# Four of eight pair steps in seven products, with two of their four weight sums made by accumulating DMAs

## The chip, the cores and the metric

One core of one Trainium2 chip runs the whole kernel. The metric is the device time of one execution in microseconds (us). The core has five engines: TensorE (PE, matrix products; PEld is its weight load), VectorE (DVE), ScalarE (ACT), GpSimd (POOL) and SyncE (SP, which here only issues DMAs). Each engine works through its own queue in order.

## The reference

One hybrid decoder layer on 256 tokens of width 2048, all in float32:

```
x = x + 1/2 * SwiGLU_1(RMSNorm(x))          # 2048 -> 5632 -> 2048
x = x + W_out [ GLA(u) ; MoBA(u) ]          # u = RMSNorm(x) @ W_in
x = x + CrossAttn(RMSNorm(x), RMSNorm(mem))
x = x + 1/2 * SwiGLU_2(RMSNorm(x))
swiglu(h) = (silu(h @ w_gate) * (h @ w_up)) @ w_down
```

The change touches only `h @ w_gate` and `h @ w_up` of the two SwiGLU blocks.

## The kernel before, in words

**Three products for one.** Float32 accuracy is had from products of a rounded type: `split_to` (L151) makes of every operand a rounded part "hi" (ACT, L152) and a rest "lo" (DVE, L153), and `mm3` (L163) issues three matmuls, hi*hi, hi*lo and lo*hi (L165 to L167). Activations are stationary (128x128), weights move (128x512). Split weights live in the buffers `whi` and `wlo`, six of each (`HIS`), each 128x2x512.

**Pairs.** A SwiGLU block has 11 column blocks of 512. The first is done plainly (`Block`), the other ten by the class `Pair`, so there are 20 pairs in the kernel. A pair computes gate and up for both halves of the tokens in eight steps, q = 0 to 7. A step loads one raw tile of 1 MB, `raw[:, 0:4]` (`load_pair`, L144: two DMAs of 512 KB on SP): places 1 and 2 hold two 128-row blocks of gate weights, places 0 and 3 two of up weights. Seven PSUM banks collect the products p1, r6, r7, p2, r5, r3, q4, and the last adds on DVE (`early`, `gates`, `ups`) turn them into the four results. `KINDS` gives the kind of each step:

- An N step splits the gate blocks and the up blocks (two `whi`/`wlo` buffers) and makes eight products of three matmuls each.
- An S step makes seven products of three matmuls each. Besides the gate blocks and one up block it needs four sums of weights, made by DVE in two tiles "st" (L232 to L235), and their splits: four `whi`/`wlo` buffers in all.

`KINDS = "NSNSNSNN"`, so steps 1, 3 and 5 are S. After the last S step, `early` (L246) takes p1, r6 and r7 out of PSUM; after step 7, `gates` and `ups` take out the others. `half_kb` tiles (`T2K` = 7 of 2 KB) hold these. `Normed.sums` (L369) prepares, once per SwiGLU block, the combined activations of each step ("eh"/"el" for S, "dh"/"dl" for N).

**What sets the order.** The text of the kernel is not the order of the queues. The framework's planner, at build time, orders each engine's queue by its own estimate of when things are ready, and sets the waits; buffers of one tag are handed out again when their last reader is done. So the sums of an S step may stand in DVE's queue well before that step's splits. Raw tiles have three buffers (`RAWS`), released when the last of a step's readers is done. POOL has nothing to do in the SwiGLU blocks.

Of the kernel before, what the change touches and what calls it, by code (L numbers as in the profile page):

```python
# [2 lines left out]

# [10 lines left out]
ALU = mybir.AluOpType  # L14
# [3 lines left out]
P = 128  # L18
# [6 lines left out]
NB = 512  # L25
# [19 lines left out]
OFF_MV = OFF_MK + BH * DH  # L45
RAWS = 3
HIS = 6
T2K = 7
KINDS = "NSNSNSNN"


@with_exitstack
def hymba_layer(ctx: ExitStack, tc: tile.TileContext, x, mem, ffn1_norm, ffn1_w_gate, ffn1_w_up,
# [3 lines left out]
    nc = tc.nc  # L57
# [10 lines left out]
    pools = {}  # L68
# [13 lines left out]
    def nm(s):  # L82
        count[0] += 1
        return f"{s}_{count[0]}"
# [35 lines left out]
    def own_tile(shape, tag, dtype=F32):  # L120
        return pools["own"].tile(shape, dtype, tag=tag, name=nm(tag))

    def tmp_tile(shape, tag, bufs=2, dtype=F32):
        return pools["tmp"].tile(shape, dtype, tag=tag, name=nm(tag), bufs=bufs)

    def half_kb(shape=(P, NB)):
        return tmp_tile(list(shape), "t2k", 8 if "mix" in pools else T2K)

    ahead = {}

    def raw_tile():
        return wp.tile([P, 4, NB], F32, tag="raw", name=nm("raw"))

    def load_raw(k0, c0, w, n=NB, step=4):

        raw = raw_tile()[:, :step, :n]
        nc.sync.dma_start(raw, w[k0 * P:(k0 + step) * P, c0:c0 + n].rearrange("(k p) n -> p k n", p=P))
        return raw

    def take_raw(k0, c0, w, n=NB, step=4):  # L140
        key = id(w), k0, c0
        return ahead.pop(key) if key in ahead else load_raw(k0, c0, w, n, step)

    def load_pair(k0, c0, wg, wu):  # L144

        raw = raw_tile()
        for dst, w in ((raw[:, 1:3, :], wg), (raw[:, 0:4:3, :], wu)):
            nc.sync.dma_start(dst, w[k0 * P:(k0 + 2) * P, c0:c0 + NB].rearrange("(k p) n -> p k n", p=P))
        return raw

    def split_to(hi, lo, src):  # L151
        nc.scalar.activation(hi, src, AF.Copy)  # L152
        nc.vector.tensor_tensor(lo, src, hi.bitcast(F32), op=ALU.subtract)  # L153

    def split_raw(raw):

        k, n = raw.shape[1:]
        bufs = 3 if "mix" in pools else HIS
        hi, lo = (tmp_tile([P, 2, NB], tag, bufs, F32R)[:, :k, :n] for tag in ("whi", "wlo"))
        split_to(hi, lo, raw)  # L160
        return [(hi[:, i, :], lo[:, i, :]) for i in range(k)]
# [7 lines left out]
    def bank(n=NB):  # L169
        return pools["mm"].tile([P, NB], F32, tag="mm", name=nm("mm"))[:, :n]  # L170

    class Block:
# [7 lines left out]
        def step(self, k0, nk=4):  # L180
            hi, lo = self.a
            k2 = k0
            while k2 < k0 + nk:
                raw = take_raw(self.w_k0 + k2, self.c0, self.w, self.n, min(4, k0 + nk - k2))
                for i in range(0, raw.shape[1], 2):
                    ws = split_raw(raw[:, i:i + 2])
                    for t in range(NT):
                        s = slice(t * P, (t + 1) * P)
                        for k, w in enumerate(ws, k2 + i):
                            mm3(self.ps[t], (hi[:, k, s], lo[:, k, s]), w, k == 0,  # L190
                                k == self.nk - 1)
                k2 += raw.shape[1]
            pump()
            if k0 + nk == self.nk:
                self.done(self.ps)

    class Pair:
# [3 lines left out]
        def __init__(self, a, wg, wu, c0):  # L201
            self.a, self.wg, self.wu, self.c0 = a, wg, wu, c0
            self.p = {n: bank() for n in ("p1", "r6", "r7", "p2", "r5", "r3", "q4")}
            self.left = {n: KINDS.count("S") + (0 if n in ("p1", "r6", "r7") else 1) *
                         KINDS.count("N") for n in self.p}
            self.total = dict(self.left)
# [11 lines left out]
        def step(self, q):  # L218
            if self.begun is None:
                self.begun = set()  # L220
            a = self.a
            raw = load_pair(2 * q, self.c0, self.wg, self.wu)
            g, u2 = raw[:, 1:3], raw[:, 3:4]
            if KINDS[q] == "N":
                gs, us = split_raw(g), split_raw(raw[:, 0:4:3])
                for name, t, ws in (("p2", 0, gs), ("q4", 1, gs), ("r3", None, us), ("r5", 1, us)):
                    for i, w in enumerate(ws):
                        x = a.diff(2 * q + i) if t is None else a.plain(t, 2 * q + i)
                        self.add(name, x, w, i == 1)
            else:  # L230
                sa, sb = (tmp_tile([P, 2, NB], "st") for _ in range(2))
                nc.vector.tensor_tensor(sa, raw[:, 1:4:2], raw[:, 0:1].to_broadcast([P, 2, NB]),  # L232
                                        op=ALU.add)
                nc.vector.tensor_tensor(sb[:, 0:1], sa[:, 0:1], u2, op=ALU.add)
                nc.vector.tensor_tensor(sb[:, 1, :], sb[:, 0, :], raw[:, 2, :], op=ALU.add)  # L235
                gs, (us,) = split_raw(g), split_raw(u2)
                sums = split_raw(sa) + split_raw(sb)
                e, o = 2 * q, 2 * q + 1
                for name, x, w in (("p1", a.plain(0, e), gs[0]), ("p2", a.plain(0, o), gs[1]),
                                   ("r3", a.comb(3, q), us),  # L240
                                   ("r5", a.comb(0, q), sums[0]), ("r7", a.comb(2, q), sums[1]),
                                   ("r6", a.comb(1, q), sums[2]), ("q4", a.plain(1, o), sums[3])):
                    self.add(name, x, w, True)
            pump()

# [28 lines left out]
    def pump():  # L274

        while behind:
            try:
                next(behind[0])
                return
            except StopIteration:  # L280
                behind.popleft()
# [60 lines left out]
    class Normed:  # L342
# [6 lines left out]
        def begin(self):  # L349
            self.hi, self.lo = (act_tile([P, KC, T], tag, F32R) for tag in ("xhi", "xlo"))  # L350
            self.ss = small.tile([P, NT, 4], F32, tag="ss", name=nm("ss"))
            if self.pairs:
                self.s = [q for q in range(KC // 2) if KINDS[q] == "S"]
                self.n = [q for q in range(KC // 2) if KINDS[q] == "N"]
                self.e = [own_tile([P, len(self.s), 4, P], t, F32R) for t in ("eh", "el")]
# [13 lines left out]
        def sums(self, q, x):  # L369

            f = tmp_tile([P, 4, P], "xg", 3)
            if KINDS[q] == "S":
                for out, x0, x1 in ((f[:, 0], x[1][:, 0], x[1][:, 1]),
# [633 lines left out]
```

## Time and profile before

| | |
|---|---|
| median of 2 runs | 1957.38 us (1956.18 to 1958.57) |
| the profiled execution, device time | 1955.91 us |
| its span, first to last instruction | 1954.2 us |
| PE busy | 1933.9 us, 99% of the span |
| DVE busy | 1410.2 us, 72% |
| ACT busy | 1019.8 us, 52% |
| POOL busy | 23.8 us, 1% |
| granted TensorE clock | 1.00 |
| read from memory | 365.50 MB |

The profile is of one execution. Busy time is the time in which an engine had an instruction in work; matmuls overlap each other at their ends, so PE's busy time shows that it never rests, and the pace is read from the starts of successive matmuls. A wait is put down to what released it.

### The profile page before, as it was taken

The page shows a single profiled execution, that of the slowest core. Times are in us where ns is not written, and L with a number is a line of the kernel's source. Part 1 is how long each engine was busy: PE and PEld are TensorE (multiplying, and loading weights), DVE is VectorE, ACT ScalarE, POOL GpSimd, SP SyncE. Part 2 cuts the span into 40 slices and gives each one's busy share as a digit, 9 for nine tenths or more (in the row PEclk, how much of TensorE's full clock was granted, in tenths as well). Part 3 has the DMA queues.
Part 4 walks back from the last instruction along what each step waited for, and adds up shares of the span by engine and source line. Part 5 has one row for each costly group of instructions (what it writes and reads, how often), then busy time and mean ns, then how long its engine had stood idle before and what let it go on. Part 6 is the DMA issues. An engine that isn't in the chain of part 4 may idle for free.

```text
span 1954.2 us, 23322 instructions
## 1 busy us (share of the span) xinstructions
PE 1933.9 (99%) x8932; PEld 1604.1 (82%) x8932; DVE 1410.2 (72%) x1726; ACT 1019.8 (52%) x1268; POOL 23.8 (1%) x52
## 2 busy tenths in 40 slices
PE   7999999999999999999999999999999999999999
PEld 6888888888888888987788888888888888888887
DVE  7788569895589755465665766979856988558873
ACT  6555445554355545635464655655534555435552
POOL 0000000000000000000000000000000000000000
PEclk9999999999999999999999999999999999999999
DMA  7565555565556636554455544656555565655663
GB/s 239 203 206 193 195 191 185 204 207 202 194 173 214 205 126 205 172 192 148 152 172 200 178 160 152 207 181 214 194 194 185 184 213 196 211 196 172 205 206 128
DMA packets 192456, 369.13 MB, mean 189 GB/s; under 512 B 8692, under 2 KB 19144, under 8 KB 192344
## 3 DMA queue, kind: packets, MB, share of 16 engines
q1 hardware_dynamic: 192344, 367.64, 56.0%
q8 instruction: 70, 1.15, 0.2%
q14 instruction: 42, 0.34, 0.0%
HBM read 365.50 MB, written 2.10 MB: 188 GB/s over the span
## 4 chain that ended last, share of the span: by engine, by line
PE 97%; DVE 1%; DMA 1%; ACT 0%; issue 0%; SPq 0%
PE mm L165 31%; PE mm L167 31%; PE mm L166 31%; PE aux L415 1%; PE aux L328 1%; DVE wlo L153 0%; DMA raw<-in_xattn_w_o_dram 0%; PE aux L746 0%; DMA raw<-in_ffn_w_gate_dram 0%; ACT whi L152 0%; PE aux L696 0%; PE aux L691 0%; PE aux L667 0%; PE aux L932 0%; PE aux L781 0%
## 5 line engine op out<-in xcount | busy, mean ns | idle before, releaser
L153 DVE TENSOR_TENSOR wlo<-raw,whi 128x1024 fp32r<-128x1024 f32 (+3 forms) x704 | 807.7, 1158 | 433.0 <-ACT whi L152 429.0
L152 ACT ACTIVATE whi<-raw 128x1024 fp32r<-128x1024 f32 (+3 forms) x704 | 698.1, 1003 | 778.7 <-PE mm L167 720.3
L165 PE MATMUL mm<-whi,xhi 128*128 128x512 f32 (+2 forms) x1356 | 528.0, 390 | 1.2 <-ACT whi L152 1.2
L166 PE MATMUL mm<-wlo,xhi 128*128 128x512 f32 (+2 forms) x1356 | 522.5, 385 | 0.7 <-DVE wlo L153 0.7
L167 PE MATMUL mm<-whi,xlo 128*128 128x512 f32 (+2 forms) x1356 | 522.2, 385 | 0.0
L167 PE MATMUL mm<-whi,biglo 128*128 128x512 f32 x864 | 336.8, 390 | 0.1
L165 PE MATMUL mm<-whi,bighi 128*128 128x512 f32 x832 | 326.3, 392 | 0.0
L166 PE MATMUL mm<-wlo,bighi 128*128 128x512 f32 x832 | 324.1, 390 | 0.0
L165 PEld LDWEIGHTS mm<-whi,xhi 128*128 128x128 f32 x1356 | 254.8, 188 | 51.0 <-ACT whi L152 2.2
L167 PEld LDWEIGHTS mm<-whi,xlo 128*128 128x128 f32 x1356 | 254.7, 188 | 50.3 <-DVE xlo L153 0.5
L166 PEld LDWEIGHTS mm<-wlo,xhi 128*128 128x128 f32 x1356 | 255.1, 188 | 48.6 <-DVE wlo L153 1.3
L167 PEld LDWEIGHTS mm<-whi,biglo 128*128 128x128 f32 x864 | 162.1, 188 | 34.5 <-DVE biglo L153 0.6
L166 PEld LDWEIGHTS mm<-wlo,bighi 128*128 128x128 f32 x832 | 156.3, 188 | 31.7
L165 PEld LDWEIGHTS mm<-whi,bighi 128*128 128x128 f32 x832 | 156.2, 188 | 31.5
L153 DVE TENSOR_TENSOR wlo<-st,whi 128x1024 fp32r<-128x1024 f32 x120 | 146.6, 1222 | 30.3 <-ACT whi L152 26.8
L152 ACT ACTIVATE whi<-st 128x1024 fp32r<-128x1024 f32 x120 | 127.2, 1060 | 66.0 <-PE mm L167 43.4
L165 PE MATMUL mm<-whi,eh 128*128 128x512 f32 x240 | 93.4, 389 | 0.0
L167 PE MATMUL mm<-whi,el 128*128 128x512 f32 x240 | 93.4, 389 | 0.0
L166 PE MATMUL mm<-wlo,eh 128*128 128x512 f32 x240 | 93.4, 389 | 0.0
L232 DVE TENSOR_TENSOR st<-raw 128x1024 f32<-128x1024 f32 x60 | 73.2, 1220 | 7.0 <-DMA raw<-in_ffn_w_up_dram 6.3
L165 PE MATMUL mm<-whi,dh 128*128 128x512 f32 x200 | 77.8, 389 | 0.0
L166 PE MATMUL mm<-wlo,dh 128*128 128x512 f32 x200 | 77.8, 389 | 0.0
(206 smaller groups left out, 1422.8 us busy)
## 6 DMA issues: line engine op xcount, KB each, us to landing
raw<-in_ffn_w_down_dram SPq DMA_DIRECT2D x88, 1024.0 KB, 5.1
raw<-in_ffn_w_gate_dram SPq DMA_DIRECT2D x162, 512.0 KB, 3.9
raw<-in_ffn_w_up_dram SPq DMA_DIRECT2D x160, 512.0 KB, 4.8
raw<-in_w_in_dram SPq DMA_DIRECT2D x40, 1024.0 KB, 5.1
raw<-in_w_out_dram SPq DMA_DIRECT2D x16, 1024.0 KB, 5.1
raw<-in_ffn_w_up_dram SPq DMA_DIRECT2D x8, 1024.0 KB, 5.2
raw<-in_ffn_w_gate_dram SPq DMA_DIRECT2D x7, 1024.0 KB, 5.2
raw<-in_w_in_dram SPq DMA_DIRECT2D x8, 688.0 KB, 4.2
```

What stands on the lines that cost most here:

```text
L152: nc.scalar.activation(hi, src, AF.Copy)
L153: nc.vector.tensor_tensor(lo, src, hi.bitcast(F32), op=ALU.subtract)
L165: nc.tensor.matmul(p, a[0], w[0], start=start, stop=False)
L166: nc.tensor.matmul(p, a[0], w[1], start=False, stop=False)
L167: nc.tensor.matmul(p, a[1], w[0], start=False, stop=stop)
L232: nc.vector.tensor_tensor(sa, raw[:, 1:4:2], raw[:, 0:1].to_broadcast([P, 2, NB]), op=ALU.add)
L328: nc.tensor.transpose(pt[:, i, :], c[:, i * P:(i + 1) * P], ident)
L415: nc.tensor.transpose(pt[:, i, :], h[t][:, i * P:(i + 1) * P], ident)
```

## The change

Step 6 becomes an S step, so that four of eight are S. In an S step, DVE makes only two sums, in one tile "st": s1 = gate block 0 + up block 0, and t2 = s1 + up block 1. The other two are made in place in the raw tile by DMAs that add to their destination, issued from POOL: up block 0 becomes t3 = up block 0 + up block 1, and gate block 1 becomes t4 = gate block 1 + t2. The second may only write once the gate blocks are split, the first once s1 is made; both must have landed before t3 and t4 are split. "st" has one buffer, not two. A fourth raw tile, of the phase's own pool, is used for every fourth load outside the mixer, and `T2K` goes from 7 to 5.

```diff
-T2K = 7
-KINDS = "NSNSNSNN"
+T2K = 5
+KINDS = "NSNSNSSN"
...
+    turns = itertools.count()
+
     def raw_tile():
+
+        if "mix" not in pools and next(turns) % (RAWS + 1) == RAWS:
+            return tmp_tile([P, 4, NB], "raw", 1)
         return wp.tile([P, 4, NB], F32, tag="raw", name=nm("raw"))
...
-                sa, sb = (tmp_tile([P, 2, NB], "st") for _ in range(2))
-                nc.vector.tensor_tensor(sa, raw[:, 1:4:2], raw[:, 0:1].to_broadcast([P, 2, NB]),
-                                        op=ALU.add)
-                nc.vector.tensor_tensor(sb[:, 0:1], sa[:, 0:1], u2, op=ALU.add)
-                nc.vector.tensor_tensor(sb[:, 1, :], sb[:, 0, :], raw[:, 2, :], op=ALU.add)
+                st = tmp_tile([P, 2, NB], "st", 1)
+                u1 = raw[:, 0]
+                nc.vector.tensor_tensor(st[:, 0], raw[:, 1], u1, op=ALU.add)
+                nc.vector.tensor_tensor(st[:, 1], st[:, 0], raw[:, 3], op=ALU.add)
+                nc.gpsimd.dma_start(u1, raw[:, 3], accum_op=ALU.add)
                 gs, (us,) = split_raw(g), split_raw(u2)
-                sums = split_raw(sa) + split_raw(sb)
+                nc.gpsimd.dma_start(raw[:, 2], st[:, 1], accum_op=ALU.add)
+                s1, t2 = split_raw(st)
+                t3, t4 = split_raw(raw[:, 0:4:2])
                 e, o = 2 * q, 2 * q + 1
                 for name, x, w in (("p1", a.plain(0, e), gs[0]), ("p2", a.plain(0, o), gs[1]),
                                    ("r3", a.comb(3, q), us),
-                                   ("r5", a.comb(0, q), sums[0]), ("r7", a.comb(2, q), sums[1]),
-                                   ("r6", a.comb(1, q), sums[2]), ("q4", a.plain(1, o), sums[3])):
+                                   ("r5", a.comb(0, q), s1), ("r6", a.comb(1, q), t2),
+                                   ("r7", a.comb(2, q), t3), ("q4", a.plain(1, o), t4)):
                     self.add(name, x, w, True)
```

## Rows read from the trace of the kernel before

**Rows 1.** The page: span, and busy us by engine
```profile
span 1954.2 us, 23322 instructions
PE 1933.9 (99%) x8932; PEld 1604.1 (82%) x8932; DVE 1410.2 (72%) x1726; ACT 1019.8 (52%) x1268; POOL 23.8 (1%) x52
```

**Rows 2.** The page: the chain that ended last, by engine
```profile
PE 97%; DVE 1%; DMA 1%; ACT 0%; issue 0%; SPq 0%
```

**Rows 3.** Waits, longest in total: who waited for whom, us, times, longest
```profile
ACT whi L152 <- PE mm L167: 763.7, 552, 8.7
```

**Rows 4.** Busy time in one pair's period: us, engines, clock, DMA share, GB/s
```profile
103.79:146.23 42.44, 42.44 (x193) 35.12 (x192) 38.00 (x42) 24.27 (x28) 0.00 (x0) 1.00 0.58 199
```

**Rows 5.** Timeline of PE, steps 4 and 5 of that pair: start, duration
```profile
126.42 0.39 PE L165 MATMUL mm<-whi,xhi 128*128 128x512 f32 x1
...
131.86 0.39 PE L165 MATMUL mm<-whi,xhi 128*128 128x512 f32 x1
...
132.54 0.39 PE L165 MATMUL mm<-whi,xhi 128*128 128x512 f32 x1
...
135.26 0.39 PE L165 MATMUL mm<-whi,eh 128*128 128x512 f32 x1
...
136.62 0.39 PE L165 MATMUL mm<-whi,xhi 128*128 128x512 f32 x1
```

**Rows 6.** DVE's groups by shape: count, busy us, mean ns, idle before
```profile
L153 DVE TENSOR_TENSOR wlo<-raw,whi 128x1024 fp32r<-128x1024 f32 x604 | 738.0, 1228 | 398.1 <-ACT whi L152 396.3
L153 DVE TENSOR_TENSOR wlo<-st,whi 128x1024 fp32r<-128x1024 f32 x120 | 146.6, 1222 | 30.3 <-ACT whi L152 26.8
L232 DVE TENSOR_TENSOR st<-raw 128x1024 f32<-128x1024 f32 x60 | 73.2, 1220 | 7.0 <-DMA raw<-in_ffn_w_up_dram 6.3 <-DVE wlo L153 0.3
L153 DVE TENSOR_TENSOR wlo<-raw,whi 128x512 fp32r<-128x512 f32 x76 | 52.1, 687 | 12.5 <-ACT whi L152 12.5
L234 DVE TENSOR_TENSOR st<-st,raw 128x512 f32<-128x512 f32 x60 | 41.2, 687 | 0.6
L235 DVE TENSOR_TENSOR st<-st,raw 128x512 f32<-128x512 f32 x60 | 41.2, 686 | 0.5
```

**Rows 7.** DMA issues: count, KB each, median us from issue to landing
```profile
raw<-in_ffn_w_down_dram SPq DMA_DIRECT2D x88, 1024.0 KB, 5.1
raw<-in_ffn_w_gate_dram SPq DMA_DIRECT2D x162, 512.0 KB, 3.9
t2k<-in_mem_dram SPq DMA_DIRECT2D x8, 256.0 KB, 6.3
out_dram<-x_sb SPq DMA_DIRECT2D x8, 256.0 KB, 2.6
```

**Rows 8.** Timeline of DVE and ACT, splits of the same pair: start, duration
```profile
114.67 1.82 DVE L153 TENSOR_TENSOR wlo<-raw,whi 128x1024 fp32r<-128x1024 f32 x2
...
123.14 3.00 DVE L153 TENSOR_TENSOR wlo<-raw,whi 128x1024 fp32r<-128x1024 f32 x3
...
129.39 1.06 ACT L152 ACTIVATE whi<-raw 128x1024 fp32r<-128x1024 f32 x1 [1.66 <-PE mm L167]
130.48 1.22 DVE L153 TENSOR_TENSOR wlo<-raw,whi 128x1024 fp32r<-128x1024 f32 x1 [1.49 <-ACT whi L152]
```

**Rows 9.** One line: duration min/median/max of `early` and the combined activations
```profile
L250 DVE TENSOR_TENSOR t2k<-mm,t2k x20: 684/685/687, 94.4 to 1873.1; 128x512 f32<-128x512 f32 x20
L377 DVE TENSOR_TENSOR xg<-xg,xg x18: 282/285/290, 15.5 to 1252.1; 128x128 f32<-128x128 f32 x18
L382 DVE TENSOR_TENSOR xg<-xg,xg x10: 417/421/425, 13.3 to 1259.2; 128x256 f32<-128x256 f32 x10
L153 DVE TENSOR_TENSOR el<-xg,eh x6: 681/686/689, 17.9 to 1254.1; 128x512 fp32r<-128x512 f32 x6
L153 DVE TENSOR_TENSOR dl<-xg,dh x10: 417/420/426, 14.9 to 1260.7; 128x256 fp32r<-128x256 f32 x10
```

**Rows 10.** Timeline around the pair's end: last add (DVE), next r5 (PE)
```profile
149.71 0.68 DVE L269 TENSOR_TENSOR t2k<-mm,t2k 128x512 f32<-128x512 f32 x1
...
151.58 0.39 PE L165 MATMUL mm<-whi,xhi 128*128 128x512 f32 x1
```

**Rows 11.** DMA queue of SP, who it waited for: us in total, times, longest
```profile
SPq L148 <- DVE wlo L153: 665.1, 146, 10.9
```

More of the change, by code (lines that the diff above doesn't have):

```diff
@@ L1 @@
 import collections
+import itertools
 from contextlib import ExitStack, contextmanager
```

## The prediction, made before the changed kernel was run

> **What bounds the kernel now.** I read the page first: PE is busy 99% of the span, DVE 72% [rows 1], and the chain that ended last is PE for 97% [rows 2]. The reader is to see that PE is not waiting for anyone: all its idle time together is 1954.2 - 1933.9 = 20.3 us. Next the waits: the longest is ACT, which makes the hi parts, waiting for PE, 763.7 us in all [rows 3]. The producers run ahead until the six `whi` buffers are full, and PE's consumption frees them. Then one pair by itself, from a DVE instruction of one pair to the same one of the next: 42.44 us, in which PE never stops, the granted clock is 1.00 (the higher level, 2.4 GHz), DVE is busy 38.00 us and POOL not at all [rows 4]. So there the PE stream sets the time, and DVE has only 4.4 us to spare.
>
> PE's pace is read from starts [rows 5]: a product (three matmuls) takes 132.54 - 131.86 = 0.68 us. The N step from 126.42 to 131.86 takes 5.44 (eight products), the S step to 136.62 takes 4.76 (seven). Three S, five N and the transposes of the pair before make the 42.44.
>
> **What is taken away.** In each of 20 pairs one N step becomes S: one product less, 0.68 us, in all 13.6 us (60 of 8932 matmuls), all on the path. That is 0.7%. As PE's whole idle time is 20.3 us, even a kernel that lost all of that as well would be 33.9 us or 1.7% faster: 2%, which is about what a measurement of this kernel tells from no change, can't be reached from PE's side.
>
> **DVE's load.** An S step before: 1.22 + 0.69 + 0.69 for sums, splits of gate 1.23, up 0.69, two of "st" 2.44, in all 6.96 us; now two sums of 0.69 (the nearest rows, 128x512), and splits 1.23 + 0.69 + 1.22 + 1.23, in all 5.75 [rows 6]. The N step that becomes S had 2 x 1.23 = 2.46. Per pair: 3 x (5.75 - 6.96) + (5.75 - 2.46) = -0.3 us. ACT gains one S step's splits for an N step's, about 2 us against the 18 us it has free [rows 4]. DVE's 37.7 us against the new period of 41.76 leave 4.1 us. So by load alone DVE stays cover; its waits are the question.
>
> **The accumulating DMAs.** 160 of them, 256 KB each, on POOL's idle queue [rows 4]. The trace of before has none. Rows for 256 KB: 2.6 us for a store with nothing beside it, 6.3 us for a load behind other loads; 512 KB more cost 5.1 - 3.9 = 1.2 us, so a second read of 256 KB would add 0.6 [rows 7]. Bounds for the landing time L, an estimate: 2.6 to 6.9 us. I take 4.5 to 5, in between, because raw loads run beside it (DMA share 0.58 [rows 4]) but on another queue, so it doesn't stand behind them as the load of 6.3 did.
>
> The Trainium skill ("DMA: Bandwidth & Descriptors", Anatomy of one DMA) gives for a DMA issued from GpSimd 2.0 us plus the bytes at 436 GB/s; by that L would be 2.6 us, and no stall would follow. No run here shows it yet.
>
> How much of L is hidden? Take the new step 6, the worst, as it follows an S step. Its gate blocks can be split when PE has used up step 4's: in the trace ACT starts at 129.39, freed by PE, and DVE ends at 130.48 + 1.22 = 131.7 [rows 8]. The DMA into gate block 1 then starts. PE begins step 6 at 136.62 [rows 5] and comes to r7, which needs t3, five products later, at 140.0. Splitting takes 1.06 on ACT and 1.22 on DVE [rows 8], so t3 and t4 must have landed at 137.7: L up to 6.0 us. The other path is the single "st": step 6's first sum waits until step 5's second DMA has read "st". Step 5's gate split ends about 125.5 (two of the three at 123.14 [rows 8]); 125.5 + L + 0.7 + L must be at most 137.7: L up to 5.8 us. Steps after an N step have more: step 3's gate split ends at 115.8 (first of the two at 114.67 [rows 8]), its r7 comes 5.44 + 4.76 - 3.4 = 6.8 us before 131.86, that is at 125.1, so L may be 7.0 us. With L of 4.5 to 5 no PE wait appears: I cost the DMAs at 0, covered by the six buffers' lead. If that cover is gone, step 6 costs up to 2 us for each us of L beyond 5.8, the other three 1 us each beyond 7.
>
> **Who stands behind the waits.** ACT's and DVE's splits of t3 and t4 wait for a landing; behind them in both queues are the next step's splits, which PE needs 4 to 6 us later (wlo of step 6 ends at 131.7, used at 136.62). POOL's DMAs are in one queue, an early one of the next step behind a late one. The planner fills DVE's wait with other work as far as its estimate of L is right.
>
> **The small edits.** `early` moves one step later, 0.69 us x 2 on DVE [rows 9], still before p1, r6 and r7 are used again in the next pair's step 1; DVE's last add of the pair ends at 150.4, 1.2 us before r5's bank is written again [rows 10], so a delay over 1.2 us there would show on PE. `T2K` = 5 is what one pair uses (three in `early`, two in `gates`; `ups` works in place): 0. Combined activations: per SwiGLU four adds of 0.29 and a split of 0.69 in place of 0.42 and 0.42 [rows 9], 1 us on DVE beside the first column block: 0 to 2 us. The raw tile of an S step is held until t3 and t4 are split, longer by L and a split less the up split of 0.7, some 5 us, and the fourth tile gives one step back, 4.8 to 5.4 us; SP's loads now wait 665.1 us in all for buffers [rows 11], early rather than late: 0. DMA traffic rises by 8 x 256 KB written, or twice that read, on the 8.4 MB of a pair (199 GB/s x 42.44 us [rows 4]): share 0.72 to 0.87, an estimate, under 1. At the phase change after cross-attention a load into the new pool's raw tile may wait for its memory: -1 to +3 us.
>
> **The sum.** The profiled execution took 1955.9 (span 1954.2): 1955.9 - 13.6 + 1 = 1943.3; the median stands 1.5 above that execution. Forecast **1945 us**, own range 1940 to 1951.
>
> **Rivals.**
> 1. *Given back at step 6* (chance 0.17). L is 6 to 6.9, at the upper end of its bounds: PE waits 0.3 to 2 us for t3 in step 6 of each pair, 6 to 40 us, giving 1950 to 1985. For it: the single "st" chains two DMAs; against: 6.3 us was measured behind other loads in one queue.
> 2. *PE waits for t3 in every S step, and the kernel is slower* (0.14). The place is r7's first matmul, the price as above. At L = 8 a pair pays 4.4 + 3 x 1 = 7.4 at most, some 5.5 if step 1, after two N steps, has slack: 110 us, 2054. It passes 2% (39 us, plus the 13.6 gained) at 2.6 us per pair, L about 7.1. For it: adding needs two reads and a write, no row shows the rate, and two may be in flight. Against: both rows of 256 KB are below 7.
> 3. *DVE's waits make it the bound* (0.10). DVE has 4.1 us per pair. If each of four S steps leaves it 2 us idle with its next work behind the blocked split, a pair takes 37.7 + 8 = 45.7, 3.9 above the new period: 78 - 13.6 gives 2022. For it: 90% load and a queue in fixed order; against: lead of 4 to 6 us, and a planner that knows the DMA. A way into this case is late descriptors, because DVE runs two-input adds nearly all the time.
> 4. *More than 2% faster* (0.02): excluded by PE's count unless the trace hides idle time.
>
> On rival 3's last point the Trainium skill ("SBUF — State Buffer", SBUF: two separate sides) says that a DMA issued from GpSimd has its descriptors written by GpSimd, which DVE's two-port modes lock out. It adds, under Who interferes with whom, that a two-input add has no such mode, and that the harmlessness for descriptors is inferred; no run here shows it yet.
>
> **How the numbers follow.** Forecast 0.57, rivals 0.17, 0.14, 0.10, 0.02. Rivals 2 and 3 lie over 2% slower except small forms of 2 and 3 (0.02). So faster 0.02, within 2% 0.76, slower 0.22. The range 1940 to 2015 holds the forecast, rival 1 and the milder 2 and 3 (about 0.07): 0.8.
>
> **What would show it.** Right: 60 matmuls fewer, a pair period near 41.8, ACT still waiting mostly for PE, DMA landings on POOL's queue under 5.8 us. Wrong: PE idle before r7 or q4 of S steps, released by ACT or DVE whose own wait is for POOL's DMA (rivals 1, 2), or by DVE busy over 95% of a pair (rival 3); or PE waiting at p2, q4, r5 of a pair's first step for late adds.

## The result, and the profile after

The changed kernel takes **2159.61 us** (2 runs, 2159.03 to 2160.18) against 1957.38 before: 1.1033 times as long, 95% interval 1.0986 to 1.1081. It is 10% slower; the forecast was 1945 us, the range ended at 2015. The profiled execution took 2160.18 us at a mean granted clock of 0.972.

The page of the changed kernel: span, busy us of each engine, and the chain that ended last.

```profile
span 2158.5 us, 24006 instructions
PE 2003.3 (93%) x8872; PEld 1622.8 (75%) x8872; DVE 1395.4 (65%) x1752; ACT 1028.0 (48%) x1308; POOL 161.5 (7%) x212
...
PE 46%; issue 33%; DMA 9%; DVE 7%; POOL 2%; ACT 2%; SPq 0%; POOLq 0%; ACTq 0%; DVEq 0%
```

The 60 matmuls are gone and DVE has a little less to do, as predicted [rows 1]. But PE now stands idle for 2158.5 - 2003.3 = 155.2 us instead of 20.3, its busy time has grown although it does less, and it is 46% of the last chain instead of 97% [rows 2].

The same kernel's waits (who waited at which line for whom: us in total, times, longest).

```profile
ACT whi L158 <- PE mm L173: 522.5, 335, 8.6
...
ACT whi L158 <- DMA raw<-st: 434.7, 72, 8.8
POOL raw L243 <- DVE wlo L159: 298.2, 64, 11.9
...
DVE st L239 <- issue: 148.7, 32, 6.4
...
PE mm L171 <- ACT whi L158: 79.8, 44, 4.7
...
PE mm L172 <- DVE wlo L159: 43.7, 54, 1.3
...
DVE st L239 <- DMA raw<-st: 26.8, 8, 5.0
```

ACT's wait for PE, the sign of producers that run ahead, has fallen from 763.7 us [rows 3]. A new one stands beside it: 434.7 us for the second accumulating DMA (t4, line 243), 72 times of 80; the other eight times the same landing releases DVE's first sum. PE in turn waits for ACT and DVE, and most of its idle time lies before the products with combined activations, r3, r5, r6 and r7 (groups of the page; behind the last bar the idle time before them):

```profile
L171 PE MATMUL mm<-whi,eh 128*128 128x512 f32 x320 | 132.3, 413 | 79.0 <-ACT whi L158 78.9
...
L172 PE MATMUL mm<-wlo,eh 128*128 128x512 f32 x320 | 136.6, 427 | 43.3 <-DVE wlo L159 43.0
```

Followed through PE's timeline, these 122.3 us all lie at r7, the product that needs t3: 67.8 us in step 6, 34.3 in step 5, 18.6 in step 3 and 1.6 in step 1.

DMA issues of the changed kernel (count, KB each, median us from issue to landing).

```profile
raw<-raw POOLq DMA_DIRECT2D x80, 256.0 KB, 4.1
raw<-st POOLq DMA_DIRECT2D x80, 256.0 KB, 5.7
```

These times count from the start of POOL's instruction, so they hold the 0.86 us that it takes there (862 ns, 854 to 872 for the second). The 6.6 us that two of the expectations below name add these a second time. The second's landings run from 3.3 to 7.8 us, the first's from 3.4 to 8.4. What goes with the length is the raw loads: 47 of the 160 landed while SP's queue of loads moved under 60 GB/s, after 3.4 us (median), 95 while it moved 150 GB/s or more, after 6.3. This is read from one trace, not tried apart.

Next, one pair in stretches (window, its length, then busy us of PE, PEld, DVE, ACT and POOL, granted clock, DMA share, GB/s): the whole pair, a stretch with hardly a wait, an idle one and the stretch behind that.

```profile
105.38:160.57 55.19, 47.76 (x189) 37.52 (x188) 37.26 (x44) 24.43 (x30) 6.89 (x8) 0.90 0.68 190
139.00:151.00 12.00, 11.27 (x51) 8.97 (x50) 5.89 (x7) 3.48 (x4) 1.72 (x2) 1.00 0.71 192
152.00:156.00 4.00, 0.06 (x1) 0.00 (x0) 0.00 (x0) 0.91 (x1) 0.00 (x0) 0.98 0.32 62
156.00:160.50 4.50, 3.84 (x8) 2.75 (x9) 4.32 (x5) 4.50 (x7) 0.00 (x0) 0.50 0.42 115
```

The pair takes 55.19 us, not 42.44 [rows 4]. Where pairs follow one another directly, the time from one to the next is 53.2 to 57.4 us in the whole kernel. DVE's 37.26 us are what was forecast (37.7), and the DMA share is 0.68, far from full.

PE around the idle stretch (start, duration, instruction, and in brackets its idle time and who ended it).

```profile
151.67 0.39 PE L173 MATMUL mm<-whi,el 128*128 128x512 f32 x1
156.20 0.79 PE L171 MATMUL mm<-whi,eh 128*128 128x512 f32 x1 [4.14 <-ACT whi L158]
...
158.48 0.63 PE L171 MATMUL mm<-whi,xhi 128*128 128x512 f32 x1
158.90 0.63 PE L172 MATMUL mm<-wlo,xhi 128*128 128x512 f32 x1
...
163.18 0.39 PE L171 MATMUL mm<-whi,xhi 128*128 128x512 f32 x1
163.41 0.39 PE L172 MATMUL mm<-wlo,xhi 128*128 128x512 f32 x1
```

PE stands at step 6's r7 ("eh" is a combined activation). It waits 4.14 us for the split. When it goes on, the granted clock is 0.50 (1.2 GHz): a matmul comes every 158.90 - 158.48 = 0.42 us instead of 0.23 until about 162.7. So this idle stretch is paid a second time behind it.

ACT over the same pair and the next: the rows in which the second DMA released it. A row holds a run of like instructions; x3 after 144.65 is the split of t3 and t4, and then step 6's gate split and up split.

```profile
131.82 4.42 ACT L158 ACTIVATE whi<-raw 128x1024 fp32r<-128x1024 f32 x5 [5.98 <-DMA raw<-st]
136.15 1.04 ACT L158 ACTIVATE whi<-st 128x1024 fp32r<-128x1024 f32 x1
...
144.65 2.52 ACT L158 ACTIVATE whi<-raw 128x1024 fp32r<-128x1024 f32 x3 [7.46 <-DMA raw<-st]
147.08 1.05 ACT L158 ACTIVATE whi<-st 128x1024 fp32r<-128x1024 f32 x1
...
155.09 2.95 ACT L158 ACTIVATE whi<-raw 128x1024 fp32r<-128x1024 f32 x3 [6.96 <-DMA raw<-st]
...
172.49 2.96 ACT L158 ACTIVATE whi<-raw 128x1024 fp32r<-128x1024 f32 x3 [5.76 <-DMA raw<-st]
...
186.36 4.42 ACT L158 ACTIVATE whi<-raw 128x1024 fp32r<-128x1024 f32 x5 [4.69 <-DMA raw<-st]
```

DVE and POOL in the middle of it.

```profile
144.62 0.69 DVE L239 TENSOR_TENSOR st<-raw 128x512 f32<-128x512 f32 x1 [5.13 <-issue]
145.35 0.69 DVE L240 TENSOR_TENSOR st<-st,raw 128x512 f32<-128x512 f32 x1
145.96 2.95 DVE L159 TENSOR_TENSOR wlo<-raw,whi 128x1024 fp32r<-128x1024 f32 x3
148.84 1.22 DVE L159 TENSOR_TENSOR wlo<-st,whi 128x1024 fp32r<-128x1024 f32 x1
```

```profile
138.05 0.86 POOL L243 DMA_DIRECT2D raw<-st  x1 [4.40 <-DVE wlo L159]
145.61 0.86 POOL L241 DMA_DIRECT2D raw<-raw  x1 [6.70 <-DVE st L239]
148.61 0.86 POOL L243 DMA_DIRECT2D raw<-st  x1 [2.14 <-DVE wlo L159]
...
166.97 0.86 POOL L243 DMA_DIRECT2D raw<-st  x1 [5.54 <-DVE wlo L159]
...
180.55 0.86 POOL L243 DMA_DIRECT2D raw<-st  x1 [1.11 <-issue]
```

Read the three together from 144.6, where step 5's second DMA has landed. Only now does ACT split t3 and t4, and only behind that step 6's gate blocks. At the same moment DVE wakes: its next instruction was step 6's first sum, which had to wait until that DMA had read the single "st", and DVE's splits stand behind it. (The row calls this wait "issue"; that it is the landing is read from the time, from the eight cases above, and from experiment 8.) At 148.61 gate block 1 is split and POOL may start step 6's own second DMA, which lands 6.5 us later, at 155.09. So the landings are links of **one chain**: 3.96 us of splits, 0.86 on POOL, 5.62 to the landing, 10.44 us for a step that PE does in 4.76 [rows 5]. Over a whole pair, from 131.82 to 186.36, the links are 12.83, 10.44, 17.40 and 13.87 us, together 54.54: that is the pair's period. Landings a pair apart must add up to the period; what makes them a chain is that no link has slack in it. In each, the landing starts the splits, DVE then works without a gap until its sum or split releases POOL's next DMAs (the second at 138.05, 148.61, 166.97 and, behind the first in POOL's queue, 180.55), and ACT starts again as the second lands. The bound has moved from PE to this loop through ACT, DVE, POOL and the DMA.

### The profile page after: what moved, and what is told of

The parts are those of the page before. It is cut to its first block, busy times and chain, and to the rows that moved or that the text cites. A ratio compares the mean times of both kernels' runs of the same rounds, so it can differ in the third digit from the quotient of the medians.

```text
span 2158.5 us, 24006 instructions
## 1 busy us (share of the span) xinstructions
PE 2003.3 (93%) x8872; PEld 1622.8 (75%) x8872; DVE 1395.4 (65%) x1752; ACT 1028.0 (48%) x1308; POOL 161.5 (7%) x212
## 4 chain that ended last, share of the span: by engine, by line
PE 46%; issue 33%; DMA 9%; DVE 7%; POOL 2%; ACT 2%; SPq 0%; POOLq 0%; ACTq 0%; DVEq 0%
PE mm L172 14%; PE mm L171 14%; PE mm L173 14%; DMA raw<-st 6%; DVE wlo L159 5%; DMA raw<-in_ffn_w_up_dram 3%; POOL raw L241 2%; ACT whi L158 1%; DVE st L239 1%; PE aux L336 1%; DVE biglo L159 0%; PE aux L423 0%; PE aux L754 0%; DMA raw<-in_ffn_w_gate_dram 0%; SPq L154 0%
## 5 line engine op out<-in xcount | busy, mean ns | idle before, releaser
L158 ACT ACTIVATE whi<-raw 128x1024 fp32r<-128x1024 f32 (+2 forms) x784 | 751.5, 992 | 965.5 <-PE mm L173 512.9
L159 DVE TENSOR_TENSOR wlo<-raw,whi 128x1024 fp32r<-128x1024 f32 (+2 forms) x784 | 882.7, 1149 | 493.5 <-ACT whi L158 490.2
L171 PE MATMUL mm<-whi,eh 128*128 128x512 f32 x320 | 132.3, 413 | 79.0 <-ACT whi L158 78.9
L172 PE MATMUL mm<-wlo,eh 128*128 128x512 f32 x320 | 136.6, 427 | 43.3 <-DVE wlo L159 43.0
L239 DVE TENSOR_TENSOR st<-raw 128x512 f32<-128x512 f32 x80 | 55.0, 688 | 175.6 <-issue 148.7
L241 POOL DMA_DIRECT2D raw<-raw x80 | 69.1, 863 | 1206.6 <-DVE st L239 972.6
L171 PEld LDWEIGHTS mm<-whi,eh 128*128 128x128 f32 x320 | 61.0, 191 | 109.4 <-ACT whi L158 98.3
L173 PE MATMUL mm<-whi,el 128*128 128x512 f32 x320 | 129.2, 404 | 0.0
L172 PEld LDWEIGHTS mm<-wlo,eh 128*128 128x128 f32 x320 | 62.1, 194 | 74.4 <-DVE wlo L159 63.7
L159 DVE TENSOR_TENSOR wlo<-st,whi 128x1024 fp32r<-128x1024 f32 x80 | 97.6, 1220 | 23.7 <-ACT whi L158 23.7
```

Of the source, the lines that this page charges most:

```text
L171: nc.tensor.matmul(p, a[0], w[0], start=start, stop=False)
L172: nc.tensor.matmul(p, a[0], w[1], start=False, stop=False)
L173: nc.tensor.matmul(p, a[1], w[0], start=False, stop=stop)
L239: nc.vector.tensor_tensor(st[:, 0], raw[:, 1], u1, op=ALU.add)
L241: nc.gpsimd.dma_start(u1, raw[:, 3], accum_op=ALU.add)
```

## The experiments

**The theories.** The first (A) puts the loss to in-order queues: the landings stop ACT and DVE, and the next step's splits behind them start the next landing late. Against it stands that the DMAs cost what they do by themselves (adding, their traffic, B, or two S steps in a row), whatever the queues; and that it isn't the DMAs at all, but DVE's load or the small edits (C). A share that comes from the clock goes with any of them. The expectations name theories by letters; behind each I say in words which one stands.

**1. No accumulating DMA.** Both lines are left out.

```diff
-nc.gpsimd.dma_start(u1, raw[:, 3], accum_op=ALU.add)
-nc.gpsimd.dma_start(raw[:, 2], st[:, 1], accum_op=ALU.add)
```

> The two adding DMAs are left out, so t3 and t4 are split from unsummed weights; everything else is as in the changed kernel (four S steps, one st buffer, fourth raw tile, T2K = 5). Theory A (the loss is the landing of the second DMA, 6.6 us after POOL starts it, in front of which ACT and then DVE stand with the next step's splits queued behind): no wait is left, 1940 to 1951 us, pair period near 41.8 us, granted clock 1.00. Rival B (the loss is DMA traffic: raw loads slowed by the adding DMAs): also 1940 to 1951. Rival C (the loss is in the buffers or in early's new place, not in the DMAs): stays above 2100 us.

Measured: 1942.58 us, 0.9927 times before (0.9907 to 0.9947). All other parts of the change, the fourth raw tile, one "st", the moved `early`, cost nothing that shows; the DMAs cost 2159.6 - 1942.6 = 217 us.

**2. The same two sums in place, on DVE.**

```diff
-nc.gpsimd.dma_start(u1, raw[:, 3], accum_op=ALU.add)
+nc.vector.tensor_tensor(u1, u1, raw[:, 3], op=ALU.add)
...
-nc.gpsimd.dma_start(raw[:, 2], st[:, 1], accum_op=ALU.add)
+nc.vector.tensor_tensor(raw[:, 2], raw[:, 2], st[:, 1], op=ALU.add)
```

> Both DMAs become in-place adds of 128x512 on DVE at the same places. DVE's load per pair rises from 37.7 to about 42.6 us (eight adds of 0.61 us pitch), just over PE's 41.8. Theory A and rival B: DVE-bound by a little, 1955 to 1985 us. Rival C: above 2100 us.

Measured: **1942.82 us**, 0.9927 (0.9912 to 0.9942), below the 1955 to 1985 expected. It is 14 us under the kernel before, clear of noise, though less than 2%. Two pairs of it by themselves, with the columns as above:

```profile
99.78:142.02 42.24, 42.24 (x192) 34.96 (x191) 41.96 (x52) 25.66 (x30) 0.00 (x0) 1.00 0.57 199
142.02:183.52 41.50, 41.50 (x188) 34.34 (x188) 41.22 (x52) 24.60 (x30) 0.00 (x0) 1.00 0.56 197
```

DVE is busy 41.96 of 42.24 us, and PE still never rests. The theory of DVE's load falls here, in the very form in which it should be worst: DVE that is nearly full costs nothing here; the DMAs in the place of the same sums cost 217 us.

**3. The two sums in place, on GpSimd.** The same edit with `nc.gpsimd.tensor_tensor`.

> Both DMAs become in-place adds of 128x512 on GpSimd, at the same places; an estimate of 1.6 us each from its 128x1024 multiply of 3.17 us. Theory A: the wait shrinks from 6.6 to under 2 us and DVE's load stays 37.7 us per pair: 1942 to 1955 us, faster than the kernel before. Rival B: the same. Rival C: above 2100. A rival of its own: GpSimd and DVE hold each other up for the whole of the adds, 13 us per pair, then DVE needs some 50 us per pair: about 2120.

Measured: 1981.82 us, 1.013 (1.0113 to 1.0146), above the 1942 to 1955 expected and far from the 2120 of its own rival. DVE's groups by shape (count, busy us, mean ns, idle before):

```profile
L159 DVE TENSOR_TENSOR wlo<-st,whi 128x1024 fp32r<-128x1024 f32 x80 | 143.8, 1798 | 29.1 <-ACT whi L158 29.1
L240 DVE TENSOR_TENSOR st<-st,raw 128x512 f32<-128x512 f32 x80 | 104.0, 1301 | 0.2
```

Beside GpSimd's adds, DVE's take 1.80 and 1.30 us instead of 1.22 and 0.69 [rows 6]. The Trainium skill ("SBUF — State Buffer", Who interferes with whom) says that a DVE instruction with two inputs in SBUF contends with a GpSimd instruction that reads SBUF; the rows agree.

**4. The first DMA alone; the second sum on DVE.**

> The first DMA (t3) stays, the second (t4) becomes an in-place add on DVE. Theory A: the first DMA starts right after s1, long before t3 is needed, and its landing of 4.1 us is hidden; DVE's load is 40.1 us per pair: 1942 to 1960 us. Rival B: half of the traffic, half of the loss, about 2050 us. Rival C: above 2100.

Measured: 2012.3 us, 1.0284 (1.0264 to 1.0305): some 50 us above the 1942 to 1960 expected. One S step of it, on DVE, POOL and ACT:

```profile
117.06 0.68 DVE L239 TENSOR_TENSOR st<-raw 128x512 f32<-128x512 f32 x1
```

```profile
118.28 0.86 POOL L241 DMA_DIRECT2D raw<-raw  x1 [15.82 <-DMA raw<-in_ffn_w_gate_dram]
```

```profile
125.86 4.42 ACT L158 ACTIVATE whi<-raw 128x1024 fp32r<-128x1024 f32 x5 [5.22 <-DMA raw<-raw]
```

The first DMA was taken for harmless, because the sum that it follows can be made early. But that sum stands late in DVE's queue, at 117.06 behind splits without a gap. It ends at 117.74, the DMA starts only at 118.28 (the row names a raw load as the last that it waited for), and ACT stands until 125.86. ACT waits 161.3 us in all for it. The same stand, by another DMA.

**5. The second DMA alone; the first sum on DVE.**

> The second DMA (t4) stays, the first (t3) becomes an in-place add on DVE. It is the one that waits for the gate split and that ACT and the next first sum wait for. Theory A2: nearly the whole loss, 2090 to 2160 us. If both DMAs count alike by traffic or by queueing behind each other on POOL: about 2010 to 2050 us, as with the first alone.

Measured: 2116.14 us, 1.0816 (1.0794 to 1.0838). Over experiment 2, the second DMA alone costs 173 us, the first alone 69, both 217: together they cost less than the sum of the two, as links of one chain would.

**6. DMAs that copy and don't add.** Only `, accum_op=ALU.add` is dropped.

> Both DMAs only copy instead of adding (same bytes written, the destination is not read), so t3 and t4 hold copies and not sums; the order of all five queues is exactly that of the changed kernel. Theory A1 (the adding is slow: it reads twice): the landing of the second DMA falls from 5.7 to under 3.5 us, and the time to 2000 to 2090 us. Theory A2 (the landing is long because the DMA is generated by GpSimd and shares the DMA engines with the raw loads): 2130 to 2165 us with nearly the same landing. A1 and A2 agree that what waits is ACT's split of t3 and t4.

Measured: 2078.28 us, 1.0617 (1.0596 to 1.0639). The time lies in the range expected for slow adding, the second landing doesn't: it was to fall under 3.5 us. The copies take POOL 0.54 us and land after 2.3 and 4.3 us (median), so adding costs 1.4 to 1.8 us of landing, 0.32 of it on POOL, and this is worth 81 us, well under half of the 217. But a mere copy in the same place still costs 2078.3 - 1942.6 = 136 us. So adding explains the smaller part.

**7. Splits of t3 and t4 moved.** They, r7 and q4 come behind the next step's gate splits and first products. The order of sums is as it was.

```diff
-                s1, t2 = split_raw(st)
-                t3, t4 = split_raw(raw[:, 0:4:2])
...
+                self.flush()          # splits t3, t4 of the last S step; r7, q4
+                s1, t2 = split_raw(st)
...
+                self.rest = (q, raw[:, 0:4:2])
```

> The DMAs stay as they are; only the split of t3 and t4 and their products r7 and q4 move behind the next step's gate splits and first products (and early with them). Theory A (ACT's in-order queue: the next step's splits stand behind a split that waits 6 to 8 us): ACT's wait for the DMA nearly vanishes, 1943 to 1975 us. Rival (the DMA's length or traffic itself sets the time, wherever the split stands): above 2080 us.

Measured: 2077.15 us, 1.0612 (1.0595 to 1.063): 82 us better, far from the 1943 to 1975 expected and 3 us under what its rival, the DMA's length by itself, was to give. Its waits (line 241 is here the first sum), and one stand of DVE and of PE:

```profile
ACT whi L158 <- DMA raw<-st: 239.7, 60, 8.9
...
DVE st L241 <- issue: 131.7, 21, 8.5
...
DVE st L241 <- DMA raw<-st: 85.8, 19, 6.0
```

```profile
143.80 0.69 DVE L241 TENSOR_TENSOR st<-raw 128x512 f32<-128x512 f32 x1 [6.61 <-issue]
...
146.40 0.79 PE L172 MATMUL mm<-wlo,xhi 128*128 128x512 f32 x1 [4.26 <-DVE wlo L159]
```

ACT's stand is nearly halved, but DVE's at the first sum, for "st" to be read, has grown from 148.7 + 26.8 to 131.7 + 85.8 us. PE no longer waits at r7 at all. It now stands at step 6's first product, 68.6 us in 20 pairs, whose split is behind DVE's sum: the landing itself is covered, the queue behind it is not. That was the second half of the chain, which the expectation left out.

**8. Two buffers for t2.** s1 and t2 get tiles of their own, t2 two of them; `T2K` is 4 to make room.

```diff
-T2K = 5
+T2K = 4
...
-                st = tmp_tile([P, 2, NB], "st", 1)
+                sums = [tmp_tile([P, NB], "s1", 1), tmp_tile([P, NB], "t2", 2)]
```

> The two DVE sums get a tile each, s1 with one buffer and t2, which the second DMA reads, with two (T2K goes to 4 to pay for it; s1 and t2 are split by 512 columns each). The next S step's first sum no longer waits for the second DMA to have read t2. The split of t3 and t4 stays where it is. Theory A2 (two queues stand at the second DMA's landing, ACT at the split of t3 and t4, DVE at the next S step's first sum): only DVE's stand goes, the chain from step 5 into step 6 loosens: 2060 to 2130 us. If ACT's stand alone makes the loss: no change, 2145 to 2165 us. If DVE's alone does: under 1990 us.

Measured: 2122.29 us, 1.0847 (1.0826 to 1.0869), 37 us better than the change. DVE's stand at the first sum is gone from its waits; ACT's is still there, 373.1 us for the second DMA, with step 6's gate split behind it:

```profile
143.30 2.52 ACT L158 ACTIVATE whi<-raw 128x1024 fp32r<-128x1024 f32 x3 [8.55 <-DMA raw<-t]
```

**9. Both, 7 and 8.**

> Both edits together: t3 and t4 split behind the next step's first products, and two buffers for t2. Theory A2: both stands at the landing go, 1945 to 1990 us. Rival (the DMAs' length keeps the raw tiles too long, so the loads come late, or the queue order puts the split early again): 2030 to 2080 us.

Measured: **1960.93 us** (6 runs, 1954.92 to 1965.65), 1.0021 (1.0004 to 1.0038). The edits give 82 and 37 us by themselves and 199 together. Each alone leaves the other way round the loop closed: moved splits leave DVE waiting for "st", a second t2 leaves ACT standing ahead of the gate blocks. One pair of it, and two of its waits:

```profile
105.06:148.46 43.40, 41.21 (x186) 33.88 (x185) 37.37 (x48) 25.17 (x34) 6.88 (x9) 1.00 0.89 245
```

```profile
ACT whi L158 <- PE mm L173: 592.0, 435, 8.7
...
ACT whi L158 <- DMA raw<-t: 139.2, 40, 6.3
...
PE aux L442 <- DVE biglo L159: 8.8, 8, 2.3
```

The same 160 accumulating DMAs, landing no sooner (5.4 and 5.7 us, median), now cost 18 us instead of 217, and the granted clock is 0.998 to 1.00 in all six runs. So nine tenths of the loss hung on what stood behind the two waits: the first theory, shown. The moved splits also let PE ask for t3 and t4 three or four products, 2 to 2.7 us, later; what that gives by itself was not tried apart, but experiment 7 has it too and still loses 135 us.

**10. Three S steps instead of four**, `KINDS = "NSNSNSNN"`, where no S step follows another.

> As changed, but step 6 is an N step again: three S steps, none next to another. Theory A: three landings per pair are still in ACT's way, but the chain of step 5 into step 6 is gone: 2020 to 2090 us. If nearly all of the loss is the two adjacent S steps (the prediction's rival 1): 1965 to 1990 us.

Measured: 2041.01 us, 1.0427 (1.0406 to 1.0448). As many S steps as before, none behind another, and still 84 us slower than before: a form with the loss and without the pair of S steps in a row.

**11. Four S steps, none behind another**, `KINDS = "SNSNSNSN"`.

> Four S steps with an N step after each of the first three and the next pair's ... S step first: kinds SNSNSNSN, so no two are adjacent, also across pairs. Theory A: four landings per pair in ACT's way, without the chain of two: 2050 to 2130 us. If adjacency is all: 1945 to 1965 us.

Measured: 2123.1 us, 1.0846 (1.0825 to 1.0868). Setting the four apart gives back 36 us of 217: two S steps in a row are not the main cause. ACT still waits 425.9 us for the second DMA. Per S step the loss is 84 / 60 = 1.4 us in experiment 10, (2123.1 - 1942.6) / 80 = 2.3 here and 217 / 80 = 2.7 in the changed kernel: the more N steps stand between S steps, the less each costs. That fits a lead which N steps build up again; it was not tried by itself.

## Why the prediction was wrong, step by step

**The step that failed** is "How much of L is hidden?", with its end, "I cost the DMAs at 0, covered by the six buffers' lead". It measured each landing by itself against PE's use of the product, and began step 6's clock at the gate split of the kernel before, where DVE ends at 131.7 [rows 8]. That time belonged to a schedule without landings. In the changed kernel step 6's gate split stands in ACT's queue behind the blocked split of step 5's t3 and t4, and ends at about 148.6, only 3.96 us after step 5's landing. A lead of buffers covers a delay once; here each landing starts the next one late, the lead is used up within the first pair (PE stands 2.66 us at the r7 of its step 6), and the loop's 54.54 us a pair replace PE's 41.76.

**"Who stands behind the waits"** named exactly this: "behind them in both queues are the next step's splits". The forecast priced it at nothing, since "the planner fills DVE's wait with other work as far as its estimate of L is right". It didn't: DVE stood 148.7 us at the first sum, ACT 434.7 us at the split. Moving just these two things took away 199 of 217 us (experiment 9).

**The landing time** was 4.5 to 5 us with bounds 2.6 to 6.9. Measured from POOL's start, the median is 5.7 for the second and 4.1 for the first, single ones up to 7.8 and 8.4. So it was sized about right, and it is not the failure: by the prediction's own price 5.7 us costs nothing, as step 6 was to stand 5.8, and experiment 9 has the same landings without the loss. What its reasoning left out is the raw loads: landings beside them were longer, though they have another queue. The Trainium skill's sum ("DMA: Bandwidth & Descriptors", Anatomy of one DMA) gave 2.6 us; with the add, the rows here differ, 4.1 and 5.7 after the issue, and the measurement decides; the plain copy of the first sum, 2.3, comes near it.

**A price left out: the clock.** Against experiment 2 the profiled span is 218.5 us longer. PE's idle time is 155.2 - 19.8 = 135 us of that, its busy time 2003.3 - 1920.2 = 83 us. Of these 83 the lower level of the clock explains some 60 us at most, an estimate: 1 - 0.972 of the 2158.5 us. Experiment 3, where PE also stops and the granted clock stays at 1.00, has 1931.9 - 1920.2 = 12 us of such growth, so part of the rest is likely that a matmul beside a gap doesn't overlap its neighbour. The prediction priced idle time at its own length. How far the clock alone sets the loss could not be tried apart from the idle time.

**The rivals.** Rival 2 had the place right (PE at r7's first matmul, in three of the four S steps) and the mechanism half: its price for each us of L came again from single landings, so its 110 us at L = 8 is half of what came at a median of 5.7. Rival 1 is refuted as the main cause by experiment 11, though step 6 has the largest share of PE's stands. Rival 3 is two things. As DVE's load it is refuted by experiment 2. As DVE idle "with its next work behind the blocked split" it named half of the loop: DVE is idle 55.19 - 37.26 = 17.9 us in the pair, not 8, and busy for 68% of it, not over 95%; what DVE stood at was the first sum. Its other road, late descriptors, doesn't show. The Trainium skill ("SBUF — State Buffer", Who interferes with whom) infers that two-input adds do not starve the writing of descriptors; POOL's steady 854 to 872 ns agree, as the 52 second DMAs whose issue lies under DVE's work take 857 to 872 and the 20 that find DVE mostly idle 859 to 867.

**What held.** 60 matmuls fewer and 13.6 us: experiments 1 and 2 stand 14.5 and 14.3 us below their runs of before. DVE's load covered by PE: held up to 41.96 of 42.24 us. The small edits at about nothing: held (experiment 1). DMA share 0.72 to 0.87, under 1: 0.68 in the pair shown, 0.89 in a pair of experiment 9 at nearly the old pace, just above the upper end.

**Left open.** Experiment 9's last 18 us. ACT still waits 139.2 us for the second DMA, but PE hardly ever before the products with combined activations (0.8 us in all). It waits 8.8 us at transposes, for DVE's splits of a block of h; one such wait, of 2.19 us, is all the idle time in the pair above (43.40 - 41.21). How that comes from the DMAs was not tried.

## What to carry to other kernels

Before giving a piece of work to a DMA, ask what stands behind the instruction that waits for the landing, in its engine's queue: if that is what starts the next DMA, the landings add up round a loop, and a lead of buffers hides it only until the lead is used up. Compare the loop's length (splits, issue, landing, per step) with the bound's pace, not one landing with one slack. And check that both ways round are cut, the reader's queue and the source's buffer; either alone leaves most of the loss.

## What the runs showed of the hardware

- After an idle stretch of 4.14 us PE came back at a granted clock of 0.50 and ran at it for some 6.5 us; over the kernel the lower level costs some 60 us at most, an estimate from the mean granted clock of 0.972, beside 135 us of idle time.
- One accumulating DMA of 256 KB within SBUF costs POOL 0.86 us and lands 3.3 to 8.4 us after its start there: 3.4 (median) where raw loads moved under 60 GB/s beside it, 6.3 where they moved 150 or more. A plain copy of that size costs 0.54 and lands after 2.3 or 4.3 (median, by place).
- A GpSimd add beside DVE's two-input adds stretches those by half to nine tenths (1.22 to 1.80 us, 0.69 to 1.30).
